# The feed-forward of an encoder layer as an up-pass and a down-pass through DRAM, with seven products down

## The chip, the core and the metric

The kernel runs on one core of a Trainium2 chip. The metric is the device time of one execution in microseconds, the median over runs. Times of single steps come from one profiled execution of the kernel before. The engines are TensorE (PE; its weight loads are listed as PEld), VectorE (DVE), ScalarE (ACT), GpSimd (POOL) and SyncE (SP), whose queue issues most of the DMA transfers.

## The reference, cut to what matters

One layer of a bidirectional encoder, applied to 2048 tokens of one request and 256 of another with the same weights, all in fp32. With D = 1024 and D_FF = 2816 the part that is changed is:

```python
x = x + concatenate([m_out, a_out], -1) @ w_out      # mixers: mLSTM heads, attention heads
h = rmsnorm(x, norm2_w)
u = centred_dwconv(h @ w_up, conv_w, conv_b)         # width 3 over positions, per channel
a, g = split(u, 2, axis=-1)                          # 2816 channels each
x = x + (silu(g) * a) @ w_down
y = rmsnorm(x, final_norm_w)
```

## The kernel before

Channels lie on the 128 partitions and tokens along the free dimension. The 2304 tokens of both requests are one row; the convolution is cut at token 2048. Phases a, b and c make the projections, the mixers and w_out; c stores x after the mixers in `x1_d` and its norm in `n2_d`, both in DRAM, and ends with the first up-products already under way. Phase d is the feed-forward.

A product in fp32 precision is made of three: each operand is split into a rounded part hi and a remainder lo (ScalarE copies hi, VectorE subtracts), and TensorE adds hi x hi, hi x lo and lo x hi in PSUM.

The up-projection is done by seven products for eight, in the Strassen-Winograd form: the weights of two channel tiles are a 2x2 matrix of quarters (`up_start`, names "11", "21", "t2", "t1", "t3", "22", "t4"), and so is the normed input of a token block (its halves of channels and of tokens, `n2_ops`). GpSimd forms the weights' sums (tw, lines 1189 to 1192); the inputs' sums are made by `n2_sums` (L1149) and put in DRAM as `n2t_d`, and `n2_load` brings the seven operands in and splits them. One call of `up` thus takes two channel tiles through seven products of 12 matmuls with up to 386 columns, into a PSUM bank each (p1, p2, p3, L1184), and u is put together by copies (ScalarE, L1200) and additions (VectorE, L1203).

Phase d loops over three blocks of 768 tokens, and in each over 11 groups of two channel tiles. A group calls `up` for the gate's two tiles and for the other branch's two. `conv` applies the width-3 convolution to each u (ScalarE L1271, VectorE L1278); five columns at a block's edge are carried over. The gate passes through silu, VectorE multiplies (L1358), and the result is split into act (L1363, L1364). Two tiles of w_down are loaded (rd, L1367) and split (wd, L1373, L1374). One group later `down` multiplies them by ordinary products: for eight channel tiles and two halves of 384 tokens, six matmuls (pd, L1322) into a bank, which VectorE adds to one of eight accumulators (L1324) that began as x. So each group's down-products lie among the next group's up-products. `finish` makes the final norm of a block: squares (ScalarE), their sums (GpSimd), rows of 1/rms by TensorE (L131, L142), a multiplication (L1312) and the store (L1313).

The order on each engine is laid out once, when the program is built, by a planner with a model of each instruction's time: an instruction is placed when its operands and a free buffer are there by the model, earlier ones in the program first. Each engine then goes through its list strictly in that order, and waits at the first instruction that isn't ready. The same holds for SP's and GpSimd's lists of DMA issues. Buffers of a tag are used in turn; a later pool in the same place waits for those instructions that used the tile that lay there.

Of the kernel before, what the change touches and what calls it, by code (L numbers as in the profile page):

```python
# [17 lines left out]
P = 128  # L18
D = 1024
# [16 lines left out]
BLK = 768  # L36
# [3 lines left out]
WU = 5  # L40
# [6 lines left out]
LAGO = 2  # L47
AB = 3
NH = 386
NW = 2 * NH + 1  # L50
DT = (0, 2 * NH, 2 * NH + BLK, T)
# [17 lines left out]
WD = 4  # L69
# [3 lines left out]
PO = 4  # L73
PB = 4
# [3 lines left out]
ZT = 3  # L78
SG = 3
RS = 2  # L80
# [914 lines left out]
def phase_c(g, sn, sp, pp, wps):  # L995
# [50 lines left out]
    def post(b, z, x, po, acc):  # L1046
        xz = x[:, 2 * z:2 * z + 2]
        nc.vector.tensor_tensor(xz, po, xz, ALU.add)
        if z % 2:
            g.st.dma_start(g.x1_d[b, :, 2 * z - 2:2 * z + 2], x[:, 2 * z - 2:2 * z + 2])  # L1050
# [26 lines left out]
    for n, b in enumerate(order):  # L1077
        x, mx = nxt
        for z in range(4):
# [14 lines left out]
            if n > 4 and sums:  # L1094

                n2_sums(g, sp, 0, sums.pop(0), tag="rn", bufs=2)
# [39 lines left out]
def n2_sums(g, pool, b, c, engs=("gpsimd",) * 4, tag="raw", bufs=RW):  # L1136


    nc = g.nc
    n = (DT[b + 1] - DT[b]) // 2  # L1140
    rs = []
    for k in range(2):
        r = pool.tile([P, D if tag == "raw" else 2 * NH], F32, tag=tag, name=f"rn{b}_{c}_{k}", bufs=bufs)[:, 0:2 * n]
        r = r.rearrange("p (h t) -> p h t", h=2)
        nc.sync.dma_start(r, g.n2_d[:, c + NCC // 2 * k, DT[b]:DT[b + 1]].rearrange("p (h t) -> p h t", h=2))
        rs.append(r)
    (b11, b12), (b21, b22) = ((r[:, 0], r[:, 1]) for r in rs)
    for eng, (o, p, q) in zip(engs, ((b11, b12, b11), (b12, b22, b12), (b22, b22, b11), (b21, b21, b22))):
        getattr(nc, eng).tensor_tensor(o, p, q, ALU.subtract)  # L1149
    for k in range(2):  # L1150
        g.st.dma_start(g.n2t_d[b, k, :, c, :, 0:n], rs[k])


def up_load(g, s1, b, jj):

    rs = [s1.tile([P, D], F32, tag="raw", name=f"ru{b}_{jj + k}", bufs=RW) for k in range(2)]
# [5 lines left out]
def up_start(g, s1, ps, ops, b, jj, rs=None):  # L1162
# [3 lines left out]
    n = (DT[b + 1] - DT[b]) // 2  # L1166
    nm = f"{b}_{jj}"
# [3 lines left out]
    t1, t2, t4 = (s1.tile([P, h], F32, tag="tmp", name=f"tw{k}_{nm}", bufs=3) for k in (1, 2, 4))  # L1171

    def bank(k):
        return ps.tile([P, 512], F32, tag="p", name=f"p{k}_{nm}", bufs=PB)[:, 0:n]

    def mul(p, k, src, add=False):

        w = s1.tile([P, 2, NCC // 2, P], F32R, tag="wu", name=f"wu{k}_{nm}", bufs=WU)
# [3 lines left out]
        for c in range(NCC // 2):  # L1182
            for i, (aa, bb) in enumerate(((0, 0), (0, 1), (1, 0))):
# [34 lines left out]
    return rest  # L1218


def phase_d(g, tc, s1, pd, ops, first):

    nc = g.nc
    ND = T // BLK
# [359 lines left out]
```

## Time and profile before

| | |
|---|---|
| median of 3 runs | 3429.08 us (3423.29 to 3429.88) |
| span of the profiled execution | 3427.2 us |
| TensorE busy | 3329.3 us, 97%, 20058 matmuls |
| VectorE, ScalarE, GpSimd busy | 2677.3, 1931.2, 1120.9 us |
| granted TensorE clock, mean | 0.990 |
| DMA, mean over the span | 118 GB/s, 404 MB |
| first up-product to last down-product | 1830 to 3411 us |

The median stands for the kernel; the profiled execution's own time is its span and the little that lies around it. A row of a group reads: line, engine, operation, tiles written and read, shape, number | busy time in us and mean ns of one | idle time of the engine just before them, with what ended it. A row of TensorE's timeline reads: start, duration of the run of like instructions, their kind and number. Matmuls overlap, so that their distance is read from start to start, not from their mean duration. A window row gives, after its length, the busy time of each engine with the number of its instructions, the granted clock, the DMA engines' busy share and their GB/s.

### The profile page before, as it was taken

To read this page: it belongs to the slowest core of one execution; us is meant where nothing else is said; L and a number is where in the kernel's file an instruction comes from. 1 tells how busy PE (TensorE), PEld (TensorE's weight loads), DVE (VectorE), ACT (ScalarE), POOL (GpSimd) and SP (SyncE) were. 2 spreads that over 40 slices of the span, in tenths; PEclk is the share of its full clock that TensorE was granted. 3 is DMA by queue.
4 is the path that set the end of the run, shared out by engine and by line. 5 is a ranking of instruction groups with operands and counts; after the bars stand their busy time and mean duration, and the time that the engine had idled before them with its cause. 6 is when DMAs were issued, how large, how long until landed. Compare 5 with 4: busy or idle time off the path is not lost. (4 is left out here: it accounts for less than half of the span.)

```text
span 3427.2 us, 55596 instructions
## 1 busy us (share of the span) xinstructions
PE 3329.3 (97%) x20058; PEld 3098.4 (90%) x20058; DVE 2677.3 (78%) x4654; ACT 1931.2 (56%) x4329; POOL 1120.9 (33%) x1328
## 2 busy tenths in 40 slices
PE   7989999999999999899999999999999999999998
PEld 6878888888888888688899999999999999999998
DVE  6885687777768788967767878789888888888776
ACT  4536666666666767655544444446444446555554
POOL 6653132213232323211244333226233224322222
PEclk9999999999999999999999999999999999999999
DMA  6765342333345444422365232223323213421221
GB/s 220 243 203 159 89 140 86 115 123 98 108 131 160 143 123 139 145 77 94 101 216 198 81 105 87 68 80 133 129 94 103 72 59 128 140 74 62 69 74 50
DMA packets 254756, 404.27 MB, mean 118 GB/s; under 512 B 32112, under 2 KB 156816, under 8 KB 254480
## 3 DMA queue, kind: packets, MB, share of 16 engines
q1 hardware_dynamic: 226576, 358.23, 32.7%
q0 software_dynamic: 11344, 33.04, 3.6%
q10 hardware_dynamic: 16560, 9.44, 0.9%
q8 instruction: 158, 2.59, 0.3%
q14 instruction: 118, 0.97, 0.1%
HBM read 316.73 MB, written 83.90 MB: 117 GB/s over the span
## 5 line engine op out<-in xcount | busy, mean ns | idle before, releaser
L1322 PE MATMUL pd<-act,wd 128*128 128x384 f32 (+1 forms) x3120 | 593.4, 336 | 23.9 <-DVE acc L1324 12.6
L1322 PEld LDWEIGHTS pd<-act,wd 128*128 128x128 f32 x3120 | 539.6, 188 | 32.6 <-DVE acc L1324 18.1
L601 DVE TENSOR_TENSOR pl<-ps,ph 128x512 fp32r<-128x512 f32 x520 | 352.7, 683 | 181.5 <-ACT ps L600 173.4
L1184 PE MATMUL pa<-nt,wut 128*128 128x386 f32 (+2 forms) x2376 | 454.3, 339 | 0.0
L599 ACT ACTIVATE ph<-ps 128x512 fp32r<-128x512 f32 x520 | 309.4, 595 | 243.5 <-PE ps L596 239.5
L1184 PEld LDWEIGHTS pa<-nt,wut 128*128 128x128 f32 x2376 | 421.6, 190 | 0.3 <-ACT u L1200 0.3
L570 DVE TENSOR_REDUCE mx<-px 128x1 f32<-128x512 f32 (+1 forms) x528 | 345.5, 670 | 74.4 <-PE px L569 72.4
L1278 DVE SCALAR_TENSOR_TENSOR y<-u,cw,y 128x768 f32<-128x768 f32 (+1 forms) x264 | 315.6, 1196 | 36.4 <-ACT y L1271 29.3
L1189 POOL TENSOR_TENSOR tw<-ru 128x512 f32<-128x512 f32 x66 | 94.1, 1425 | 732.5 <-DMA ru<-w_up 558.5
L613 PE MATMUL pv<-ph,v 128*128 128x512 f32 (+1 forms) x1040 | 319.4, 401 | 1.0 <-ACT ph L599 0.8
L600 ACT ACTIVATE ps<-ps 128x512 f32<-128x512 f32 x520 | 310.3, 597 | 0.0
L1200 ACT ACTIVATE u<-pa 128x386 f32<-128x386 f32 (+2 forms) x264 | 128.3, 486 | 320.9 <-PE pa L1184 320.7
L1324 DVE TENSOR_TENSOR acc<-pd,acc 128x384 f32<-128x384 f32 (+1 forms) x544 | 280.3, 535 | 35.5 <-PE pd L1322 34.1
L1041 PEld LDWEIGHTS po<-cmx,wo 128*128 128x128 f32 x1728 | 220.7, 191 | 8.2 <-DVE mmx L931 0.6
L1041 PE MATMUL po<-cmx,wo 128*128 128x256 f32 x1728 | 224.2, 284 | 0.4 <-DVE mmx L931 0.4
L595 PE MATMUL ps<-qq,kk 128*128 128x512 f32 x520 | 215.5, 416 | 4.2 <-DVE mx L570 2.4
L569 PE MATMUL px<-kk,qq 128*128 128x512 f32 (+1 forms) x528 | 202.8, 413 | 6.0 <-DVE mx L570 2.9
L596 PE MATMUL ps<-qm,kl 65*128 65x512 f32 x520 | 206.7, 399 | 0.0
L759 PE MATMUL mj<-mn,wm 128*128 128x256 f32 x1296 | 203.0, 289 | 2.8 <-ACT og L773 1.9
L759 PEld LDWEIGHTS mj<-mn,wm 128*128 128x128 f32 x1296 | 187.1, 193 | 19.8 <-ACT og L773 2.0
L769 PEld LDWEIGHTS mv<-wm,mn 128*128 128x128 f32 x1296 | 182.8, 190 | 18.4 <-ACT qb L765 2.5
L769 PE MATMUL mv<-wm,mn 128*128 128x256 f32 x1296 | 196.5, 285 | 1.0 <-ACT qb L765 0.9
(288 smaller groups left out, 7266.6 us busy)
## 6 DMA issues: line engine op xcount, KB each, us to landing
ru<-w_up SPq DMA_DIRECT2D x132, 512.0 KB, 3.4
mn<-n_d SPq DMA_DIRECT2D x216, 256.0 KB, 3.4
rd<-w_down SPq DMA_DIRECT2D x66, 512.0 KB, 3.6
n_d<-n1T SPq DMA_DIRECT2D x18, 1024.0 KB, 5.6
dm<-nm_d POOLq DMA_DIRECT2D x72, 256.0 KB, 4.1
mjn<-n_d SPq DMA_DIRECT2D x72, 256.0 KB, 3.3
mvn<-n_d SPq DMA_DIRECT2D x72, 256.0 KB, 3.1
q_d<-qz SPq DMA_DIRECT2D x18, 512.0 KB, 3.7
```

The source lines that it names most:

```text
L570: nc.vector.tensor_reduce(s.mx[:, t, z0:z0 + 1], ps[:, 0:w], AX.X, ALU.max)
L599: nc.scalar.activation(ph, ps, AF.Exp)
L600: nc.scalar.activation(ps, ps, AF.Exp)
L601: nc.vector.tensor_tensor(pl, ps, f32(ph), ALU.subtract)
L613: nc.tensor.matmul(s.pv[0:HD if k in (1, 3) else P, 0:N], v, p, start=(kp == 0 and k == 0), stop=(2 * kp + 2 == s.nk and k == 5))
L759: nc.tensor.matmul(pj[:, o], s.w[c][:, a, o * P:(o + 1) * P], nT[c][:, :, h, :], start=(c + o + k == 0), stop=(c == NCC - 1 and k == 2 and ...
L769: nc.tensor.matmul(pv[:, o], nT[c][:, o, a, :], s.w[c][:, h, 256:512], start=(c + o + k == 0), stop=(c == NCC - 1 and k == 2 and o == 1))
L1041: nc.tensor.matmul(po[:, o], wo[z // 2][c][:, a, n], mx[c][:, h, :], start=(c == 0 and k == 0), stop=(c == NCC - 1 and k == 2))
L1184: nc.tensor.matmul(p, w[:, aa, c, :], ops[k][:, c, bb, 0:n], start=c == 0 and i == 0 and not add, stop=c == NCC // 2 - 1 and i == 2, skip_ ...
L1278: nc.vector.scalar_tensor_tensor(y[:, s:e], u[:, s + k:e + k], cw[:, k, jj:jj + 1], y[:, s:e], ALU.mult, ALU.add)
L1322: nc.tensor.matmul(po, wds[j][c // 4][:, aa, c % 4 * P:(c % 4 + 1) * P], acts[j][:, bb, z0:z1], start=(j == 0 and k == 0), stop=(j == len( ...
L1324: nc.vector.tensor_tensor(accs[c][:, z0:z1], po, accs[c][:, z0:z1], ALU.add)
```

## The change

Phase d becomes two passes with the activations in DRAM between them.

**Up-pass (`phase_u`).** Two blocks of 1152 tokens instead of three of 768, with the same 11 groups. Operands and products are 572 or 580 columns wide in place of 382 to 386; each product is made in two halves (z) of 286 or 290 columns in two PSUM banks, so that one call of `up` has 7 x 24 matmuls. The weights' buffers are 4, not 5, and the raw weights lie in two pools. There are no down-products. The gated result of a group is a 2x2 matrix (two channel tiles by two halves of 576 tokens); GpSimd forms four sums (t1, t2, t3, t4) and stores all seven operands in `a_d` from its own DMA queue. `n2_sums` works in quarter pieces and through GpSimd's queue as well, in buffers shared with t1, t2 and t4.

**Down-pass (`phase_e`).** Seven products, each over 11 pairs of rows of w_down (p), for four tiles of 128 output channels (half of D) and 1152 columns (half of each block), in three column groups of 384 (z). For each product (i) and column group, TensorE goes through the 11 pairs with 12 matmuls each into two tiles of two PSUM banks; `update` copies or adds them to one or two of four accumulators (`quad`). Activations are loaded by fours of pairs in four buffers, and split; weights are loaded in two buffers (dw), split into 13 (w), and fetched during a product's last column group for the next product. The accumulators begin without x; x is loaded and added by GpSimd once an accumulator is nearly done (`resid`), and the norm's squares follow. The last product's last column group goes by halves of its channels.

Four of the seven weight operands are sums. GpSimd forms them inside the down-pass, in three buffers of their own (ds): t1 and t2 for all 11 pairs while the first product runs (`sums_a`: three loads, an addition, a subtraction, two stores to `s_d`), t3 and "22" while the second runs (`sums_b`: four loads, one of them of t2 from `s_d`, two subtractions, two stores). They are loaded again from `s_d` as weights. The loads are issued by SP, the stores by GpSimd.

`x1_d` is laid out by channel tile and token, and w_down is read once for the unsummed weights and again for the sums, not once per block.

```diff
-BLK = 768
+BLK = 1152
-WU = 5
+WU = 4
-NH = 386
+NH = 580
-DT = (0, 2 * NH, 2 * NH + BLK, T)
+DT = (0, 2 * NH, T)
+HB = BLK // 2
+TW = T // 2
+NP = NFC // 2
+CG = 384
+WR = 13
+TR = 4
+DS = 3
+TG = 4
+WA = 2
...
@@ up_start, mul
-        for c in range(NCC // 2):
-            for i, (aa, bb) in enumerate(((0, 0), (0, 1), (1, 0))):
-                nc.tensor.matmul(p, w[:, aa, c, :], ops[k][:, c, bb, 0:n], start=c == 0 and i == 0 and not add,
-                                 stop=c == NCC // 2 - 1 and i == 2, skip_group_check=add)
+        for z in range(2):
+            for c in range(NCC // 2):
+                for i, (aa, bb) in enumerate(((0, 0), (0, 1), (1, 0))):
+                    nc.tensor.matmul(p[:, z], w[:, aa, c, :], ops[k][:, c, bb, z * m:z * m + m],
+                                     start=c == 0 and i == 0 and not add, stop=c == NCC // 2 - 1 and i == 2,
+                                     skip_group_check=add)
...
@@ phase_u, a group
+            def store(k, gi, t):
+                nc.gpsimd.dma_start(g.a_d[gi // TG][DOPS.index(k), :, gi % TG, b * HB:(b + 1) * HB], t)
...
+                for y, yg in zip(yas, ygs):
+                    nc.vector.tensor_tensor(y, y, yg, ALU.mult)
+                b11, b12, b21, b22 = (y[:, k * HB:(k + 1) * HB] for y in yas for k in range(2))
+                store("11", gi, b11)
+                nc.gpsimd.tensor_tensor(t1, b12, b11, ALU.subtract)
+                nc.gpsimd.tensor_tensor(t2, b22, t1, ALU.subtract)
+                for k, t in (("t2", t2), ("21", b21), ("t1", t1)):
+                    store(k, gi, t)
+                nc.gpsimd.tensor_tensor(b12, b22, b12, ALU.subtract)
+                nc.gpsimd.tensor_tensor(t4, b21, t2, ALU.subtract)
+                for k, t in (("t3", b12), ("22", b22), ("t4", t4)):
+                    store(k, gi, t)
...
+def phase_e(g, tc, pd):
...
+        def halves(t, src):
+            lo, hi = t[:, 1], t[:, 0]
+            nc.scalar.activation(hi, src, AF.Copy)
+            nc.vector.tensor_tensor(lo, src, f32(hi), ALU.subtract)
...
+        def sums_a(p):
+            a, b = raw(0, 1, p, "ds", DS), raw(1, 1, p, "ds", DS)
+            nc.gpsimd.tensor_tensor(b, a, b, ALU.add)
+            nc.gpsimd.dma_start(g.s_d[SUM["t1"], p], b)
+            c = raw(0, 0, p, "ds", DS)
+            nc.gpsimd.tensor_tensor(c, b, c, ALU.subtract)
+            nc.gpsimd.dma_start(g.s_d[SUM["t2"], p], c)
+
+        def sums_b(p):
+            a, b = raw(0, 0, p, "ds", DS), raw(0, 1, p, "ds", DS)
+            nc.gpsimd.tensor_tensor(b, a, b, ALU.subtract)
+            nc.gpsimd.dma_start(g.s_d[SUM["t3"], p], b)
+            a, b = raw(1, 0, p, "ds", DS), saved("t2", p)
+            nc.gpsimd.tensor_tensor(b, a, b, ALU.subtract)
+            nc.gpsimd.dma_start(g.s_d[SUM["22"], p], b)
+
+        def weight(i, p):
+            k = DOPS[i]
+            w = sw.tile([P, 2, h], F32R, tag="w", name=f"we{k}_{p}", bufs=WR)
+            if k in SRC:
+                r = raw(*SRC[k], p, "dw", 2)
+            else:
+                r = sy.tile([P, h], F32, tag="dw", name=f"dw{k}_{p}", bufs=2)
+                nc.sync.dma_start(r, g.s_d[SUM[k], p])
+            halves(w, r)
+            return w
...
+        def acts(i, z, q):
+            p0, p1 = TS[q]
+            t = sx.tile([P, 2, TG, CG], F32R, tag="t", name=f"te{DOPS[i]}_{z}_{q}", bufs=TR)[:, :, 0:p1 - p0]
+            nc.sync.dma_start(f32(t[:, 1]), g.a_d[q][i, :, :, z * CG:(z + 1) * CG])
+            halves(t, f32(t[:, 1]))
+            return t
...
+        for i, k in enumerate(DOPS):
+            for z in range(G3):
+                ps = [banks(g, pd[(g.nbank + 1) // 2 % 2], f"e{k}_{z}_{m}")[:, :, 0:CG] for m in range(2)]
...
+                for p in range(NP):
+                    if p % TG == 0:
+                        fetch_t(1)
+                    mul(p, range(4))
+                    if i == 0 and z == 0 or z == G3 - 1:
+                        fetch_w(1)
+                    n = (i * G3 + z) * NP + p
+                    if i == 0 and n % 2 == 0 and n < 2 * NP:
+                        sums_a(n // 2)
+                    if i in (1, 2) and (n - G3 * NP) % 3 == 0 and n < 6 * NP:
+                        sums_b((n - G3 * NP) // 3)
+                    if late and p % 3 == 2:
+                        late.pop(0)()
+                while late:
+                    late.pop(0)()
+                for m in range(2):
+                    update(m)
```

More of the change, by code (lines that the diff above doesn't have):

```diff
@@ L1211, in rest @@
         mul(p1, "t3", a21, True)
-        copy(u22, p1)
-        add(u22, u22, u21)
+        add(u22, p1, u21)
         mul(p3, "22", t4, True)
@@ L1410, in body @@
         dram("mix_d", [NB, P, NCC, BT])
-        dram("x1_d", [NB, P, NCC, BT])
+        dram("x1_d", [P, NCC, T])
+        g.a_d = [dp.tile([7, P, min(TG, NP - p), TW], F32, name=f"a_d{p}") for p in range(0, NP, TG)]
+        dram("s_d", [4, NP, P, D // 2])
         dram("q_d", [NT, P, 8, P])
```

323 lines of the change are left out of this document (185 added, 138 removed).

## The prediction

> **What bounds the kernel now.** The page comes first, its busy times and its chain of waits, then the stretch that the change rewrites, which begins with the first product of the up-projection at 1830 us and whose last down-product ends at 3411 us.
>
> ```profile
> span 3427.2 us, 55596 instructions
> PE 3329.3 (97%) x20058; PEld 3098.4 (90%) x20058; DVE 2677.3 (78%) x4654; ACT 1931.2 (56%) x4329; POOL 1120.9 (33%) x1328
> PE pa L1184 12%; PE pd L1322 12%; PE pc L1184 6%; PE pb L1184 3%; DVE y L1278 1%; DVE acc L1324 1%; DVE wut L1181 1%; DMA ru<-w_up 1%; PE po L1041 1%; DVE wu L1181 1%; DMA rn<-n_d 1%; DVE act L1364 1%; DVE wd L1374 1%; DMA n2t_d<-rn 1%; DVE y L1358 1%
> ...
> core 0: us, PE busy (x) PEld busy (x) DVE busy (x) ACT busy (x) POOL busy (x), PEclk, DMA share, GB/s
> 1830.00:3411.00 1581.00, 1551.10 (x8898) 1540.74 (x8896) 1299.58 (x1796) 821.77 (x1629) 526.58 (x355) 1.00 0.28 93
> 3411.00:3428.00 17.00, 4.81 (x22) 4.08 (x20) 6.06 (x18) 3.51 (x10) 3.78 (x6) 0.58 0.36 125
> ```
>
> The chain of waits that ended last runs through the feed-forward's products pa, pb, pc (up) and pd (down). TensorE is busy for 1551 of those 1581 us at full clock. VectorE has 18% to spare, the DMA engines 72%. So the feed-forward is bound by TensorE, and its time is the number of matmuls times the distance between two starts, plus some 30 us of holes and a tail of 17 us. The groups give the numbers, TensorE's timeline the distances.
>
> ```profile
> L1322 PE MATMUL pd<-act,wd 128*128 128x384 f32 x2976 | 575.5, 339 | 23.9 <-DVE acc L1324 12.6 <-DVE act L1364 6.3 <-ACT act L1363 3.5
> L1322 PE MATMUL pd<-act,wd 128*128 128x256 f32 x144 | 17.9, 281 | 0.0
> L1322 PE MATMUL pd<-act,n 128*128 128x256 f32 x72 | 12.4, 284 | 0.0
> L1322 PE MATMUL pd<-nt,n 128*128 128x256 f32 x72 | 12.3, 280 | 0.0
> ...
> 1817.05 13.56 PE L1041 MATMUL po<-cmx,wo 128*128 128x256 f32 x111
> ...
> 2200.51 2.28 PE L1184 MATMUL pa<-nt,wut 128*128 128x386 f32 x12
> 2202.63 2.27 PE L1184 MATMUL pc<-nt,wut 128*128 128x386 f32 x12
> 2204.74 2.08 PE L1322 MATMUL pd<-act,wd 128*128 128x384 f32 x11
> 2206.66 2.30 PE L1184 MATMUL pa<-nt,wut 128*128 128x386 f32 x12
> ...
> L245 PE MATMUL pj<-w_a,n1T 128*128 128x288 f32 x24 | 3.3, 296 | 0.0
> ```
>
> A matmul lasts 0.34 us in the rows, but the next starts long before its end. From start to start: 386 columns 2.12/12 = 0.177 us; 384 columns 1.92/11 = 0.1745 us; 256 columns (13.56 - 0.28)/110 = 0.121 us; 288 columns, from a window in the first projection, (3.3 - 0.3)/23 = 0.130 us.
>
> **The change, part by part.**
>
> *Down-products.* Now 2976 matmuls of 384 and 288 of 256 columns: 519 + 35 = 554 us. With seven products: 7 x 11 row pairs x 4 column tiles x 3 halves' products x 3 column groups = 2772 of 384, 484 us. **-70 us.**
>
> *Up-products.* Two blocks instead of three, and each product is cut in two PSUM banks. Now 3 blocks x 22 x 7 x 12 = 5544 matmuls at 0.177 = 980 us; then 2 x 22 x 7 x 24 = 7392 of 286 or 290 columns. By the 288 row that is 7392 x 0.130 = 961 (-19); by a line through the 256 and 386 rows 0.1347 us, 996 us (+16). The line is measured on whole runs and at two widths, the 288 row is rounded to 0.1 us, so I stay between them, nearer to the line: 0.133 us, **+4 us** (-19 to +16).
>
> *Holes that go.* The down matmuls' 23.9 us of waiting in their row is for VectorE's accumulators and for the activations' splits; both lie worst at the two block changes:
>
> ```profile
> 2320.00:2355.00 35.00, 29.13 (x152) 27.54 (x151) 35.00 (x38) 17.75 (x32) 23.90 (x13) 0.95 0.33 105
> 2850.00:2945.00 95.00, 84.84 (x472) 83.25 (x471) 85.59 (x113) 58.24 (x118) 54.50 (x37) 0.96 0.36 119
> ```
>
> 6 and 10 us are lost there, with VectorE busy without a break in the first. The 544 accumulator additions (row L1324 below) become 42 wide ones. **-24 us.**
>
> *Holes that the up-pass gets.*
>
> ```profile
> L1324 DVE TENSOR_TENSOR acc<-pd,acc 128x384 f32<-128x384 f32 (+1 forms) x544 | 280.3, 535 | 35.5 <-PE pd L1322 34.1
> L1278 DVE SCALAR_TENSOR_TENSOR y<-u,cw,y 128x768 f32<-128x768 f32 (+1 forms) x264 | 315.6, 1196 | 36.4 <-ACT y L1271 29.3 <-ACT yc L1276 5.7
> L1271 ACT ACTIVATE y<-u,cw 128x768 f32<-128x768 f32 x132 | 134.8, 1021 | 33.9 <-DVE y L1358 31.2 <-DVE u L1203 2.5
> L1200 ACT ACTIVATE u<-pa 128x386 f32<-128x386 f32 x88 | 42.9, 487 | 101.9 <-PE pa L1184 101.8
> L1363 ACT ACTIVATE act<-y 128x768 fp32r<-128x768 f32 x65 | 54.7, 841 | 94.6 <-DVE y L1358 57.7 <-PE pd L1322 37.0
> L1364 DVE TENSOR_TENSOR act<-y,act 128x768 fp32r<-128x768 f32 x65 | 77.9, 1199 | 1.0 <-ACT act L1363 1.0
> L1373 ACT ACTIVATE wd<-rd 128x512 fp32r<-128x512 f32 x124 | 72.0, 618 | 9.1 <-PE pd L1322 9.0
> L1374 DVE TENSOR_TENSOR wd<-rd,wd 128x512 fp32r<-128x512 f32 x124 | 94.2, 779 | 0.0
> ...
> L1184 PE MATMUL pc<-n,wu 128*128 128x386 f32 (+2 forms) x792 | 153.7, 341 | 1.0 <-ACT u L1200 1.0
> L1184 PE MATMUL pc<-nt,wut 128*128 128x386 f32 (+2 forms) x792 | 151.7, 338 | 0.9 <-POOL nt L1129 0.9
> ...
> L856 POOL DMA_DIRECT2D dm<-nm_d x72: 536/607/659, 278.4 to 1406.8; - x72
> ```
>
> One block change is left, with operands 1.5 times as long and no down-product to run meanwhile: 10 us as in the longer of the two windows (3 to 20). At its start, four late operands of 1.5 times the size are awaited where 0.9 us is lost now: 4 us (0 to 15). In between I charge nothing. A product now lasts 24 x 0.133 = 3.2 us, which covers the evacuation of the bank it doesn't use (u, 0.49 us for 386 columns, so 0.74 for 580, behind at most one convolution step of 1.02 x 1.5 us). VectorE's conv steps (1196 ns for 768 columns) are 1.8 us for 1152; four of them, seven weight splits (0.8), three additions (0.8) and one product of the two branches (1.8) are some 17 of the 22.4 us of an up call. GpSimd gets, for each group of two calls, 4 sums of the activations beside its 8 of the weights (1.4 to 1.8 us for 512 columns, rows further down) and 7 DMA issues of 0.6 us: 25 of 45 us. **+14 us.**
>
> *The seam.* The down-pass's first activations are loaded where the last operands of the up-pass lay, its first weights where a u buffer lay. So after the last up matmul: either a load of 0.79 MB (7.0 us for 512 KB in the dense first stage, row below), a copy and a subtraction of 1536 columns (about 1.7 and 2.4 us), or the last convolution (0.7 + 1.5 + 3.6), a load (3.4, mn below) and a weight's splits (1.4). Both make 11 to 12 us; nothing else is there for TensorE: 12 us (8 to 20). Then the first eleven weights pass through two buffers, a load and two splits, 5.1 us, for each two, against 2 x 12 x 0.1745 = 4.2 us of matmuls: 6 us (0 to 13). **+18 us.**
>
> *The down-weights' sums*, the largest unknown. While the first two products run (2 x 3 x 11 x 12 x 0.1745 = 138 us), GpSimd forms 44 sums of 128x512 through three buffers: load, add, store to DRAM, and later the load again.
>
> ```profile
> q1 hardware_dynamic: 226576, 358.23, 32.7%
> ...
> mn<-n_d SPq DMA_DIRECT2D x216, 256.0 KB, 3.4
> dm<-nm_d POOLq DMA_DIRECT2D x72, 256.0 KB, 4.1
> n2t_d<-rn SPq DMA_DIRECT2D x8, 386.0 KB, 2.7
> ...
> x<-xT SPq DMA_DIRECT2D x16, 512.0 KB, 7.0
> mn<-n_d SPq DMA_DIRECT2D x24, 256.0 KB, 5.1
> ...
> L1191 POOL TENSOR_TENSOR ru<-ru,ru 128x512 f32<-128x512 f32 x64 | 112.5, 1757 | 0.0
> L1189 POOL TENSOR_TENSOR tw<-ru 128x512 f32<-128x512 f32 x64 | 91.5, 1430 | 729.2 <-DMA ru<-w_up 555.1 <-DVE acc L1324 114.7 <-DVE wu L1181 22.1
> ...
> 1738.53 2.44 SPq L1145 DMA_DIRECT2D rn<-n_d  x2
> 1749.84 0.32 SPq L1145 DMA_DIRECT2D rn<-n_d  x1
> ```
>
> (The second mn row is of the first 260 us, where the DMA engines move 223 GB/s.) In a round of the first kind a buffer is held for load + sum + store: at the least 3.4 + 1.4 + 2.7 = 7.5 us, at the most 5.1 + 1.8 + 4.1 plus waiting in line, some 12 us; the nearest thing in the trace, the rn rounds of load, subtractions and store through two buffers, starts anew after 11.3 us. I take 10.5 us, so eleven rounds 115 us. The last sum is wanted some 90 us after the start (69 for the first product, 21 into the second). **+25 us** (0 to 50). A second count agrees: in these 138 us 13 MB of activations (22 x 128 x 1152 x 4 bytes), 9.2 MB of weights (35 of 0.262 MB), and 14.4 and 17.3 MB for the sums (11 x 5 and 11 x 6 transfers) move, 54 MB; queue q1's row gives 358.23/(0.327 x 3427) = 320 GB/s at full engines, so 168 us, 30 more than TensorE needs.
>
> Here 256 KB land in 4.1 us from GpSimd's queue and in 3.4 us from SP's, and the sum above uses the 4.1. [...]
>
> *Norms and tail.* The norms take a single PSUM tile out of the pair rotation, so that the next column group's second tile waits for one addition, some 1 us (a bank pair's addition of 768 columns, twice the 0.54 us of row L1324): five times, +5 us (3 to 10). The tail keeps its squares, row sums, power, eight multiplications and stores, but leaves the last squares to TensorE's row sums, where GpSimd is now busy for 3.78 of the last 17 us: -3 us (0 to -4).
>
> Sum: -70 + 4 - 24 + 14 + 18 + 25 + 5 - 3 = **-31 us**. The profiled execution spans 3427.2 us, the median of the runs is 3429.1, 1.9 us around it. 3427.2 - 31 + 1.9 = 3398; I say **3400 us**, 0.8% less.
>
> **The rivals.** About 0.2%, 7 us, is what a measurement of this kernel can tell from no change.
>
> *The sums are hidden.* If the list of sums runs ahead of need, or its traffic spreads over the later products, where the DMA engines have room, the 25 us and most of the seam's 18 fall away: 3400 - 33 = 3367 us. For it: two of the four sums aren't used before the fourth and sixth product, and at 7.5 us a round the first kind is done in 83 us, before the 90. Against it: the 54 MB in 138 us need more than 320 GB/s.
>
> *SP's queue is tied to the sums* (slower). SP issues loads in a fixed order and waits at the head for a free buffer:
>
> ```profile
> SPq L1367 <- DVE wd L1374: 291.0, 32, 15.5
> ```
>
> It stood 9 us each time here, harmless as the loads are early. In the down-pass the loads of activations and weights stand behind the sums' loads. If the order was laid out for quick rounds, 22 rounds of 11.3 us take 249 us where TensorE needs 138; the activations in flight (three of four buffers) cover 25 us once. So 86 us instead of 25: 3461 us. It decides as soon as a round lasts more than (138 + 25)/22 = 7.4 us and the order puts each round ahead of the loads needed in its time; that the first half holds is likely, the second no row shows.
>
> *The up-pass alone has holes.* If each of the 44 up calls loses 1 us at a PSUM bank that the copy hasn't freed, 3444 us. Against it: 1.0 us of such waiting in the whole row of pc<-n,wu now, for 0.9 for the other, and 3.2 us of cover.
>
> **How the numbers follow.** Forecast 0.46 (own range 3382 to 3425, so 0.43 of it faster); hidden sums 0.21, faster; SP tied 0.22, of which 0.17 slower and 0.05 none to tell; holes in the up-pass 0.11, 0.07 slower. Faster 0.64, same 0.12, slower 0.24. The range reaches to the hidden case's better half and to the tied case: 3360 to 3461.
>
> **What would show it.** TensorE's distance for 290 columns at 0.130 to 0.135 us and for the down-products 0.1745; 7392 and 2772 of them. A hole of about 12 us before the first down-product. In the first two down-products, holes of together 25 us ended by weights (w) that came from the summed DRAM tiles; none in the last four beyond the norms. If the holes are ended by activations or by weights that are no sums, SP was tied. If TensorE's busy time falls by less than 60 us, the matmul prices were wrong, and with them the forecast.

## The result, and the profile after

| | before | changed |
|---|---|---|
| median | 3426.78 us (4 runs) | 3455.87 us (3452.22 to 3459.66, 4 runs) |
| ratio, 95% interval | 1 | 1.0086 [1.0072, 1.0101] |
| span of the profiled execution | 3427.2 us | 3454.7 us |
| TensorE busy, matmuls | 3329.3 us, 20058 | 3284.3 us, 21402 |

The change makes the kernel 0.9% slower. 3400 us was forecast; the time lies in the range (3360 to 3461), on the wrong side of the kernel before. The page of the changed kernel, in the same parts as before:

```profile
span 3454.7 us, 57226 instructions
PE 3284.3 (95%) x21402; PEld 3050.8 (88%) x21402; DVE 2469.8 (71%) x3748; ACT 1774.1 (51%) x3702; POOL 1427.5 (41%) x1651
PE pa L1197 7%; PE et L1478 5%; PE pc L1197 4%; PE pb L1197 2%; DMA ds<-w_down 2%; DMA s_d<-ds 2%; PE e L1478 1%; DMA te<-a_d 1%; DMA dst<-s_d 1%; DVE y L1295 1%; DMA dw<-w_down 0%; POOL ds L1362 0%; POOL ds L1370 0%; DVE we L1345 0%; POOL sm L1429 0%
L1478 PE MATMUL et<-tet,wet 128*128 128x384 f32 x1584 | 285.3, 340 | 15.4 <-ACT wet L1344 11.0
L1043 PE MATMUL po<-cmx,wo 128*128 128x256 f32 x1728 | 224.2, 284 | 25.0 <-DVE cx L1050 24.6
L1478 PE MATMUL e<-te,we 128*128 128x384 f32 x1188 | 215.7, 341 | 27.5 <-ACT we L1344 21.2
```

TensorE is busy for 45 us less, but the span is 27.5 us longer. The chain of waits now has DMA transfers in it that weren't there: the loads and stores of the sums (ds, s_d). The last three rows name three places where TensorE stands: a product of w_out in phase c (po, 25 us), and down-products with unsummed (e, 27.5) and summed weights (et, 15.4). The windows show where, first of the kernel before in the 40 us ahead of its up-products, then of the changed one:

```profile
1790.00:1830.00 40.00, 39.34 (x331) 39.14 (x330) 22.58 (x44) 10.45 (x21) 16.57 (x13) 1.00 0.57 189
```

```profile
1790.00:1830.00 40.00, 14.75 (x104) 14.32 (x103) 17.71 (x25) 9.82 (x16) 17.98 (x21) 0.70 0.88 280
1830.00:1881.00 51.00, 38.13 (x310) 37.30 (x308) 14.97 (x29) 9.27 (x13) 14.52 (x13) 0.90 0.45 145
1881.00:2885.00 1004.00, 987.25 (x7318) 983.95 (x7319) 827.89 (x658) 506.10 (x842) 610.18 (x474) 0.99 0.32 108
2885.00:2906.00 21.00, 1.71 (x7) 1.48 (x6) 15.30 (x12) 9.96 (x13) 4.82 (x6) 0.56 0.64 215
2906.00:3175.00 269.00, 245.55 (x1342) 239.02 (x1342) 108.08 (x84) 72.80 (x81) 117.85 (x106) 0.96 0.76 257
3175.00:3441.00 266.00, 258.44 (x1491) 257.48 (x1489) 137.83 (x139) 73.48 (x72) 81.35 (x45) 0.98 0.50 162
```

The 1004 us of the up-pass and the last 266 of the down-pass are nearly dense. Most of the time goes in the 91 us around phase c's end, in the 21 us between the passes, and in the 269 us of the first products of the down-pass. TensorE's timeline has the holes (in brackets: idle time before, and what ended it):

```profile
1798.53 2.79 PE L1197 MATMUL pb<-n,wu 128*128 128x290 f32 x19
1825.93 19.49 PE L1043 MATMUL po<-cmx,wo 128*128 128x256 f32 x149 [24.61 <-DVE cx L1050]
...
1862.82 3.39 PE L1197 MATMUL pa<-nt,wut 128*128 128x290 f32 x24
1867.40 0.61 PE L133 MATMUL rs_c<-ones,cacc 128*128 128x2 f32 x4 [1.19 <-POOL cacc L1059]
1869.11 0.71 PE L144 MATMUL rs_c<-ident,rcol_c 128*128 128x128 f32 x4 [1.10 <-POOL rcol_c L137]
1880.12 0.61 PE L1197 MATMUL pc<-nt,wut 128*128 128x290 f32 x1 [10.30 <-ACT nt L1130]
...
2878.79 3.34 PE L1197 MATMUL pc<-n,wu 128*128 128x286 f32 x24
2881.97 3.33 PE L1197 MATMUL pa<-nt,wut 128*128 128x286 f32 x24
2904.59 8.90 PE L1478 MATMUL e<-te,we 128*128 128x384 f32 x41 [19.29 <-ACT we L1344]
```

SP's timeline at the same places (the time at which a load or store left):

```profile
1795.72 0.33 SPq L1165 DMA_DIRECT2D ru<-w_up  x1
1810.32 3.57 SPq L1067 DMA_DIRECT2D n_d<-cx  x4
1816.97 6.00 SPq L1034 DMA_DIRECT2D cx<-xT  x4
...
1871.54 1.93 SPq L1067 DMA_DIRECT2D n_d<-cx  x2
1873.64 2.69 SPq L1129 DMA_DIRECT2D nt<-n2t_d  x4
...
2885.33 3.12 SPq L1392 DMA_DIRECT2D te<-a_d  x4
2901.42 0.81 SPq L1349 DMA_DIRECT2D dw<-w_down  x2
```

SP issues nothing from 1796 to 1810, then four stores of normed tokens (n_d<-cx), and only behind them the x of phase c's next block, for which TensorE stands 24.6 us. What SP waited for between 1795 and 1881, and in the first products of the down-pass (2880 to 3180):

```profile
SPq L1067 <- DMA rn<-n_d: 15.0, 3, 10.6
```

```profile
SPq L1349 <- DMA s_d<-ds: 68.6, 27, 5.6
SPq L1349 <- DMA s_d<-dst: 32.9, 9, 5.4
SPq L1349 <- DVE y L1295: 12.2, 1, 12.2
```

At 1796 a store of normed tokens waits for GpSimd's loads (rn) of the inputs' sums. They read other tokens of the same DRAM tensor `n2_d`: no data passes between the two. In the down-pass SP stands 101 us for the stores of the sums, whose three buffers it wants to load again, and 12 us for the last convolution's u, which lay where the first weights go.

### The profile page after: what moved, and what is told of

Read it like the earlier page. It is cut to its first block, busy times and chain, and to the rows that moved or that the text cites. A ratio compares the mean times of both kernels' runs of the same rounds, so it can differ in the third digit from the quotient of the medians.

```text
span 3454.7 us, 57226 instructions
## 1 busy us (share of the span) xinstructions
PE 3284.3 (95%) x21402; PEld 3050.8 (88%) x21402; DVE 2469.8 (71%) x3748; ACT 1774.1 (51%) x3702; POOL 1427.5 (41%) x1651
## 5 line engine op out<-in xcount | busy, mean ns | idle before, releaser
L1197 PE MATMUL pa<-nt,wut 128*128 128x290 f32 (+1 forms) x3168 | 448.9, 298 | 5.5 <-ACT u L1215 4.5
L1197 PEld LDWEIGHTS pa<-nt,wut 128*128 128x128 f32 x3168 | 433.8, 191 | 6.9 <-ACT u L1215 5.4
L572 DVE TENSOR_REDUCE mx<-px 128x1 f32<-128x512 f32 (+1 forms) x528 | 345.3, 670 | 73.6 <-PE px L571 71.4
L1295 DVE SCALAR_TENSOR_TENSOR y<-u,cw,y 128x1152 f32<-128x1152 f32 (+1 forms) x176 | 338.3, 1922 | 25.4 <-ACT yc L1293 12.1
L1478 PE MATMUL et<-tet,wet 128*128 128x384 f32 x1584 | 285.3, 340 | 15.4 <-ACT wet L1344 11.0
L1478 PEld LDWEIGHTS et<-tet,wet 128*128 128x128 f32 x1584 | 279.1, 191 | 19.4 <-ACT wet L1344 12.4
L1043 PE MATMUL po<-cmx,wo 128*128 128x256 f32 x1728 | 224.2, 284 | 25.0 <-DVE cx L1050 24.6
L1478 PE MATMUL e<-te,we 128*128 128x384 f32 x1188 | 215.7, 341 | 27.5 <-ACT we L1344 21.2
L1478 PEld LDWEIGHTS e<-te,we 128*128 128x128 f32 x1188 | 210.9, 192 | 30.8 <-ACT we L1344 22.0
L615 PE MATMUL pv<-pl,v 128*128 128x512 f32 x520 | 190.5, 399 | 0.0
```

The source lines that it names most:

```text
L572: nc.vector.tensor_reduce(s.mx[:, t, z0:z0 + 1], ps[:, 0:w], AX.X, ALU.max)
L615: nc.tensor.matmul(s.pv[0:HD if k in (1, 3) else P, 0:N], v, p, start=(kp == 0 and k == 0), stop=(2 * kp + 2 == s.nk and k == 5))
L1043: nc.tensor.matmul(po[:, o], wo[z // 2][c][:, a, n], mx[c][:, h, :], start=(c == 0 and k == 0), stop=(c == NCC - 1 and k == 2))
L1197: nc.tensor.matmul(p[:, z], w[:, aa, c, :], ops[k][:, c, bb, z * m:z * m + m], start=c == 0 and i == 0 and not add, stop=c == NCC // 2 - 1 ...
L1295: nc.vector.scalar_tensor_tensor(y[:, s:e], u[:, s + k:e + k], cw[:, k, jj:jj + 1], y[:, s:e], ALU.mult, ALU.add)
L1478: nc.tensor.matmul(ps[m // 2][:, m % 2], w[:, aa, m * P:(m + 1) * P], t[:, bb], start=p == 0 and n == 0, stop=p == NP - 1 and n == 2)
```

## The experiments

| run | edit | median, us | ratio to before, 95% interval |
|---|---|---|---|
| e1 | `n2_d` as two tensors | 3439.23 | 1.0032 [1.0022, 1.0043] |
| e2 | no sums | 3424.67 | 0.9982 [0.9973, 0.9991] |
| e3 | e1 and e2 | 3401.55 | 0.9919 [0.9901, 0.9936] |
| e4 | e1, sums in the up-pass | 3421.10 | 0.9974 [0.9963, 0.9985] |
| e5 | e4, places of late operands | 3418.95 | 0.9973 [0.9962, 0.9983] |
| e6 | e4, places of the down-pass | 3422.90 | 0.9988 [0.9978, 0.9997] |
| e7 | e4, late loads in GpSimd's queue | 3410.94 | 0.9949 [0.9934, 0.9964] |
| e8 | e5, e6, e7 | 3415.57 | 0.9962 [0.9949, 0.9975] |
| e9 | e7, places and order at the seam | 3395.84 | 0.9916 [0.9902, 0.9930] |
| e10 | e9, four raw weight buffers | 3397.83 | 0.9916 [0.9904, 0.9929] |
| e11 | e9, sums in the down-pass again | 3425.52 | 1.0002 [0.9992, 1.0012] |
| e12 | e11, sums' loads in GpSimd's queue | 3434.47 | 1.0017 [1.0007, 1.0028] |
| e13 | e11, six buffers for the sums | 3385.24 | 0.9879 [0.9863, 0.9894] |
| e14 | e12, six buffers for the sums | 3408.02 | 0.9944 [0.9932, 0.9957] |
| e15 | the changed kernel, six buffers | 3425.98 | 0.9997 [0.9988, 1.0006] |

### The store that waits for loads of other tokens, and the sums (e1 to e4)

e1 cuts `n2_d` at the token where the blocks part, so that stores of the second block touch another tensor than the loads of the first:

```diff
-        dram("n2_d", [P, NCC, T])
+        g.n2_d = [dp.tile([P, NCC, DT[k + 1] - DT[k]], F32, name=f"n2_d{k}") for k in range(2)]
```

> Changed kernel, but n2_d is two DRAM tiles, cut at token 1160, where the two blocks of the up-pass meet. Theory A (false wait): in the changed kernel the stores of the sixth token block's norm stand in SP's list behind GpSimd's loads for the input sums, which read the same DRAM tile but other tokens; SP waits from 1796 to 1810 us, the next x is loaded late, and TensorE stands still for 24.6 us. With two tiles the stores wait for nothing: 20 to 28 us faster than the changed kernel, 3428 to 3436 us. Theory B (the sums themselves are late): the hole moves to the first product with a summed operand, whose last sums are stored at 1821 us in any case: 0 to 8 us faster, 3448 to 3456.

e2 leaves the four sums out (`sums_a`, `sums_b`); the summed weights are replaced by an unsummed quarter of w_down:

```diff
-                    if i == 0 and n % 2 == 0 and n < 2 * NP:
-                        sums_a(n // 2)
-                    if i in (1, 2) and (n - G3 * NP) % 3 == 0 and n < 6 * NP:
-                        sums_b((n - G3 * NP) // 3)
```

> Changed kernel without the down-weights' sums: the four summed operands are replaced by an unsummed quarter of w_down, so the down product isn't computed rightly; loads, splits and matmuls of the down-pass stay. Theory S (the sums bind the first two products): the holes of the first 270 us of the down-pass are theirs, 25 to 35 us faster, 3421 to 3431. Theory W (the weights' two buffers and the DMA latency bind): the holes stay, 0 to 10 us faster, 3446 to 3456.

e3 has both edits.

> Both of the above: two DRAM tiles, and no down-weights' sums (the down product is not computed rightly). If the two holes are independent, the gains add up: with A and S 45 to 63 us faster than the changed kernel, 3393 to 3411; with B and W 0 to 18.

e4 has e1's edit and makes the sums in the up-pass's second block, one pair of rows in each of its 11 groups, in the buffers of t1, t2 and t4, with loads and stores in GpSimd's queue:

```diff
+            def wsums(p):
+                ...
+                nc.gpsimd.tensor_tensor(w11, w01, w11, ALU.add)
+                nc.gpsimd.dma_start(g.s_d[0, p], w11)
+                ...
             for gi, gr in enumerate(groups):
+                if b == ND - 1:
+                    wsums(gi)
```

> Two DRAM tiles for n2_d, and the down-weights' sums made by GpSimd in the second block of the up-pass, one row pair per group, through the three buffers of the activations' sums, with 4 loads and 4 stores on GpSimd's queue instead of 7 and 4. With theories A and S, and GpSimd's 46% of idle time there as cover: 40 to 60 us faster than the changed kernel, 3396 to 3416, and faster than the kernel before. If GpSimd's list is delayed by waits for its own DMA transfers, the up-pass loses 0.5 to 2 us in each of 11 groups, 5 to 20 us of it.

Since e2 and e3 leave sums out, they don't compute the layer. Against the changed kernel's 3455.9, e1 gains 16.6 us, e2 31.2 and e3 54.3: more than the sum of the two. The first hole is gone in e1; TensorE's timeline there, at phase c's end:

```profile
1812.46 7.95 PE L1043 MATMUL po<-cmx,wo 128*128 128x256 f32 x65
...
1847.87 0.71 PE L144 MATMUL rs_c<-ident,rcol_c 128*128 128x128 f32 x4 [0.75 <-POOL rcol_c L137]
1860.20 0.61 PE L1200 MATMUL pc<-nt,wut 128*128 128x290 f32 x1 [11.63 <-ACT nt L1133]
```

So the wait for tokens that were never shared is shown as the cause of the 24.6 us. The hole of 10.3 us behind it stays, and is 11.6 here. e4, which computes everything, lies 34.8 us below the changed kernel and is 0.3% faster than the kernel before. It stays 19.6 us above e3: the sums aren't free in the up-pass either, whose last product starts at 2875.41 us in e4 and at 2857.91 in e3.

### The late operands at the start of the up-pass (e5, e7)

e5 only changes the order in which the late operands' places are taken:

```diff
-        late = n2_ops(sl, 0, ("t4", "t1", "t3", "22"))
+        late = n2_ops(sl, 0, ("t4", "22", "t1", "t3"))
```

> e4 with one more edit: the four late operands' places are ordered t4, 22, t1, t3 (t1, the first one used, then no longer lies over the last norm's accumulator, so its load waits for no GpSimd instruction). Theory P (the place holds the load back): the first late load leaves SP at about 1838 instead of 1849.7 us, the hole of 11.0 us in front of the first product on it falls to 3 to 4, and the time is 3411 to 3415. Theory Q (SP's list is what holds it back: the last norm's two stores stand ahead of it, and they leave at 1847.5): the load leaves at 1849 to 1850 as in e4, the hole stays at 10 to 12 us, and the time is 3419 to 3423.

e7 keeps the places and puts the eight loads in GpSimd's queue:

```diff
-            n2_load(g, late, 0, k, engs=e)
+            n2_load(g, late, 0, k, engs=e, q="gpsimd")
```

> e4 with one more edit: the eight loads of the late operands stand in GpSimd's queue instead of SP's; their places are as in e4. Theory Q (SP's list): they pass the last norm's stores and leave at 1844 to 1845 us, right behind GpSimd's power of that norm, the hole falls from 11 to 6 to 7 us, the time is 3416 to 3418. Theory P (place): as in e4, since t1's place is let go only by that norm's last instruction; the hole stays at 9 to 12 us, the time is 3419 to 3423. Both agree that without the power's wait it would be shorter still.

SP's timeline in e5:

```profile
1849.80 1.93 SPq L1070 DMA_DIRECT2D n_d<-cx  x2
1851.89 3.40 SPq L1132 DMA_DIRECT2D nt<-n2t_d  x4
```

The place made no difference: e5's time is e4's within 2.2 us. The loads stand in SP's list behind the last norm's stores, and leave 2.1 us after them, as in e4 (1847.50 and 1849.73). In e7 TensorE's hole is half as long:

```profile
1850.13 0.71 PE L144 MATMUL rs_c<-ident,rcol_c 128*128 128x128 f32 x4 [0.76 <-POOL rcol_c L137]
1855.92 0.61 PE L1200 MATMUL pc<-nt,wut 128*128 128x290 f32 x1 [5.08 <-ACT nt L1133]
```

and the time falls by 10.2 us, 4 more than this hole gave back (11.04 us in e4). The traces show where the 4 us lie: from 1856 to 2340 us TensorE does 3546 matmuls in e7 and 3512 in e4, 34 x 0.135 = 4.6 us more work in the same time. Why the first block runs denser is not shown; each edit also makes the planner lay out all lists anew, so that differences of a few us can come from elsewhere.

### The seam between the passes (e6, e8, e9, e10)

e6 places the raw weights' and the operands' buffers over the up-pass's early operands:

```diff
+        sb = st.enter_context(tc.tile_pool(name="e_b", bufs=1, reuse_waits="tile"))
+        ... dw ...
+        sx = st.enter_context(tc.tile_pool(name="e_t", bufs=1, reuse_waits="tile"))
+        ... te ...
         sw = st.enter_context(tc.tile_pool(name="e_w", bufs=1, reuse_waits="tile"))
```

> e4 with one more edit: in the down-pass the two buffers of raw down-weights and the four of its operands are placed first, over the up-pass's early operands, and not behind the accumulators, over the buffers of its last convolutions. Theory M (the 19 us hole between the passes is a wait for a place in SBUF): the first weight load leaves SP 13 to 16 us earlier, the hole shrinks to 4 to 7 us, the time is 3405 to 3410. Theory L (the hole is the latency of load, copy and subtraction behind the last products, whatever the place): the hole stays above 15 us and the time is 3418 to 3422.

e8 has the edits of e5, e6 and e7.

> e4 with the edits of e5, e6 and e7 together. If the place and the list each hold the late operands back and lifting one alone uncovers the other, the late loads leave at 1834 to 1838 us, that hole is 1 to 4 us, and with the seam at 4 to 7 us the time is 3395 to 3402 (e4 less 8 less 13). If the hole in front of the late operands is set by the sums of the normed tokens, whose last round ends at 1828, or by the splits into high and low parts behind the loads, it stays at 8 to 11 us and the time is that of e6.

e6 is no faster than e4, and e8 is 4.6 us above e7 alone. TensorE's and then ScalarE's timeline in e6:

```profile
2895.90 5.55 PE L1506 MATMUL e<-te,we 128*128 128x384 f32 x22 [15.90 <-ACT we L1372]
...
2908.09 4.29 PE L1506 MATMUL e<-te,we 128*128 128x384 f32 x12 [4.17 <-ACT we L1372]
```

```profile
2894.66 0.66 ACT L1302 ACTIVATE y<-u,yc,cw 128x1 f32<-128x1 f32 x2 [5.74 <-DVE y L1298]
2895.24 0.61 ACT L1372 ACTIVATE we<-dw 128x512 fp32r<-128x512 f32 x1
```

SP had issued the first weights' loads much earlier:

```profile
2860.99 0.82 SPq L1377 DMA_DIRECT2D dw<-w_down  x2
```

Yet the copy of the first (we<-dw) stands in ScalarE's list behind two one-column corrections of the last convolution, which wait for VectorE. The hole went from 19.1 to 15.9 us, and a second of 4.2 us followed. The buffer's place was one lock; the order in the lists was the next. e9 opens both, on top of e7: residuals' buffers too over early operands, the accumulators over the convolution's, and the first fetch ahead in the planner's order:

```diff
-        fetch_w(WA)
-        fetch_t(2)
+        with tc.high_priority(offset=MPRI):
+            fetch_t(1)
+            fetch_w(WA)
+        fetch_t(1)
```

> e7 with a seam edit that reaches further than e6's: the raw weights', residuals' and operands' buffers of the down-pass lie over the up-pass's early operands, the split weights over its late ones, the accumulators over the convolution's buffers; and the first operand and the first two weights are given a high priority, so that their copies stand ahead of the last convolution's end in ScalarE's and VectorE's lists. Theory I (in e6 the hole stayed at 16 us since the copy of the first weight stood behind the last convolution on ScalarE): the first down-product starts 3 to 7 us after the last up-product instead of 19, a second hole of 2 to 6 us follows at the third weight, and the time is 3398 to 3404 (e7's 3411 less 7 to 13). Theory J (ScalarE and VectorE owe the last group's convolution and the first splits some 18 us of work whatever the order, and what is done first only moves the hole): the first hole falls, but together the holes of the first 60 us of the down-pass stay within 4 us of e7's, and the time is 3407 to 3412.

```profile
2873.21 0.62 PE L1510 MATMUL e<-te,we 128*128 128x384 f32 x2 [2.63 <-ACT we L1374]
2875.33 6.98 PE L1510 MATMUL e<-te,we 128*128 128x384 f32 x24 [1.51 <-DVE te L1375]
```

TensorE's timeline in e9: 19.1 us have become 2.6 and 1.5. The time falls by 15.1 us against e7. e10 has more raw buffers on top, and its time is e9's within 2 us:

```diff
-            sb.tile([P, h], F32, tag="dw", name=f"place_dw{k}", bufs=2)
+            sb.tile([P, h], F32, tag="dw", name=f"place_dw{k}", bufs=4)
```

> e9 with four buffers of raw down-weights instead of two. If the first weights of the down-pass are held by the round trip of a raw buffer (load some 2 us, copy, subtraction, free again), this takes 2 to 5 us from e9; if by ScalarE's and VectorE's lists, it is e9 within 2 us.

This is no clean test of the buffers: in e10's trace the first weight's copy (we) again comes late on ScalarE, with a hole of 14.2 us in front of the first down-product, while the up-pass happens to end 4.9 us earlier. A raw weight's load, expected at some 2 us, landed in 2.9 us in e4 (median of 19, 2900 to 3180). From the start of the last up-product to the start of the last 38 matmuls of the down-pass it is 507 us in e10, 503 in e9 and 516 in e7.

### What the sums cost in the down-pass (e11 to e15)

e11 is e9 with the sums where the change has them: e4's `wsums` is gone, `sums_a` and `sums_b` are back.

> e9 with the down-weights' sums left where the change has them, in the first products of the down-pass, in their own buffers: what the sums cost there once the waits of the other parts are mended. Theory S (the sums' own price, by GpSimd's rounds and the loads in SP's queue): 3412 to 3422, e9 plus 13 to 20, as the changed kernel with own tiles stood 18 to 38 above the variants with the sums in the up-pass or left out. Theory T (the sums cost little; what they showed was the seam's waits made longer): e9 plus 0 to 6.

It is 29.7 us slower than e9, more than either theory gave: the price is the sums' own. In the down-pass it is larger still. The sums had cost e9 17 us in the up-pass, whose last product starts at 2867.25 us there and at 2850.24 in e11; from that start to the start of the last 38 down-products it is 503 us in e9 and 549 in e11. In e12 their loads are taken off SP's queue:

```diff
-            nc.sync.dma_start(r, g.w_down[0, ...])
+            (nc.gpsimd if tag == "ds" else nc.sync).dma_start(r, g.w_down[0, ...])
```

> e11 with one more edit: the sums' own loads, of raw down-weights and of the one saved sum, stand in GpSimd's queue instead of SP's; the sums, their buffers and their place in the first products are as in e11, and so are the bytes. Theory V (SP's list is tied to the sums: the loads of the products' own weights and activations stand behind the sums' loads, and these wait at the head of the queue for the store of the round before): TensorE's stalls in the first products fall, and the time is 3397 to 3407, 19 to 29 below e11. Theory R (the transfers' rate: the sums raise the stretch from some 150 to 250 GB/s and each transfer lands later): 3418 to 3428 as e11. In between, both.

It is not faster but 9 us slower. SP's longest waits there, from 2860 to 3200 us, are for summed weights that are to be loaded (L1393), and none is for the sums' buffers, whose loads it no longer issues:

```profile
SPq L1393 <- DMA s_d<-ds: 124.1, 16, 12.5
```

So the list of SP alone is not the cause, and the rate of the transfers or the pace of a round were left. e13 and e14 double the buffers at the same bytes, at the price of one split weight:

```diff
-WR = 13
-DS = 3
+WR = 12
+DS = 6
```

> e11 with six buffers for the sums instead of three and twelve for the split weights instead of thirteen. In e11 SP's loads for a round wait for the stores of the round before (81 us in 28 waits). If this pace (load, add, store, load into the same buffer) is what the sums cost: rounds overlap, the stalls of the second product fall by half or more, the time is 3400 to 3412, 14 to 26 below e11. If it is the rate of the transfers or the one weight buffer less: 3420 to 3432.

> e12 with the same six and twelve buffers: the sums' loads are in GpSimd's queue. If e12 lost by the pace of the rounds alone (its second product waited 35 us in eight waits for summed weights), the rounds are now quicker and SP's queue is free of them: 3396 to 3408. If by the rate: 3420 to 3435.

Windows of the second product in e11, and then in e13:

```profile
2950.00:3025.00 75.00, 64.20 (x336) 61.41 (x335) 31.50 (x24) 17.23 (x19) 25.90 (x26) 0.94 0.73 243
```

```profile
2950.00:3025.00 75.00, 75.00 (x435) 75.00 (x433) 40.96 (x31) 21.49 (x24) 39.94 (x38) 1.00 0.97 335
```

e13 is 40.3 us below e11. With 335 GB/s in place of 243 TensorE is full: the rate was a consequence of the rounds, not their limit. e13 even beats e9, where the sums lie in the up-pass, by 10.6 us: its last up-product starts 15 us earlier, and from there on it takes 506 us against 503. e14 gains 26 against e12, and stays 23 above e13: with six buffers SP's queue was the better one. The last run makes these two constants the only edit of the changed kernel.

> The changed kernel with two constants changed and nothing else: six buffers for the sums instead of three, twelve for the split weights instead of thirteen. If the three buffers are what the sums cost in the changed kernel too: as e2, which left the sums out, 3422 to 3430, some 25 to 34 below the changed kernel's 3455.9 and no slower than before. If the price came with the waits at the seam, which this leaves as they are: 3440 to 3452.

It is 29.9 us faster than the changed kernel, and level with the kernel before. The first sum of each round in the changed kernel from 2905 to 2990 (number: shortest, median and longest ns, first and last start), and in e15 from 2885 to 2990:

```profile
L1362 POOL TENSOR_TENSOR ds<-ds,ds x7: 1278/1286/2678, 2909.4 to 2981.6; 128x512 f32<-128x512 f32 x7
```

```profile
L1362 POOL TENSOR_TENSOR ds<-ds,ds x11: 1273/1284/1679, 2910.2 to 2983.8; 128x512 f32<-128x512 f32 x11
```

A round takes 72.2/6 = 12.0 us through three buffers, and 73.6/10 = 7.4 us through six. (Over all eleven rounds of t1 and t2, whose last starts at 3020.5 in the changed kernel, it is 11.1 us; the rounds of t3 and "22" take 12.7 us, in e15 7.6.) The windows of the first 269 us, in e15:

```profile
2900.00:3169.00 269.00, 266.13 (x1511) 263.77 (x1512) 135.13 (x100) 83.74 (x92) 124.54 (x108) 0.99 0.79 272
```

1511 matmuls where the changed kernel had 1342: 169 x 0.1724 = 29 us. That is the gain within a few us (the hole at the seam is 16.0 us long here, not 19.3). The sums now cost next to nothing: e2, which left them out, has a median 1.3 us lower, and by the two ratios it is some 5 us faster, with intervals that just overlap. From the start of the last up-product to the start of the last 38 down-products it is 551 us in the changed kernel, 518 in e15 and 520 in e2.

## Why the prediction was wrong

*Matmuls: right.* 290 columns take (3.39 - 0.29)/23 = 0.135 us, 286 columns (2881.97 - 2878.79)/24 = 0.1325, 384 columns 75/435 = 0.1724; 0.133 and 0.1745 were used. The counts, 7392 and 2772, came out. By these distances the up-products are some 5 us dearer than forecast and the down-products some 6 us cheaper. The text wanted TensorE's busy time to fall by 60 us, or the matmul prices were wrong. It fell by 45, and they weren't: e13 has the same matmuls and is busy for 3267.5 us, 62 less than before. So the same matmuls were busy for 16.8 us more in the changed kernel, at a mean granted clock of 0.978 against e13's 0.987, and this was a bad test.

*The step that failed* is a term that the sum puts at nothing. The part on what is moved prices the down-weights' sums, but not the sums of the inputs at the end of phase c. The change makes these 1.5 times as long, cuts them in halves, moves them to GpSimd's queue and needs a fifth token block before they can start; so they run on into the stretch where SP stores the next blocks. The wait of those stores left TensorE idle for 24.6 us, against nothing in the sum. e1 shows it; taken alone it gave back 16.6 us, and 23.1 with the sums of the weights left out (e3 against e2). In e1 the last up-product starts 19.0 us earlier, but the down-pass with its waits for sums is 3.9 us longer.

*Holes that the up-pass gets.* The start was 4 us (0 to 15): measured are the holes of 1.19, 1.10 and 10.30 us and the first product's short ones. The size of the operands was seen, but not that their loads stand behind the norm's stores in SP's list (e5, e7). The block change was 10:

```profile
2362.00:2410.00 48.00, 37.77 (x259) 35.96 (x257) 45.89 (x27) 27.40 (x37) 34.75 (x15) 0.96 0.53 186
2410.00:2885.00 475.00, 472.26 (x3549) 471.80 (x3550) 370.13 (x319) 250.19 (x464) 252.63 (x198) 0.99 0.26 91
```

These windows of the changed kernel give 48 - 259 x 0.1325 = 14 us, and 475 - 3549 x 0.1325 = 5 us for the rest of the block: so the block change took 4 us more than forecast. In between nothing was charged; 5 us were lost there, and 481 - 3512 x 0.135 = 7 us in the first block (1881 to 2362). At 12 us instead of 44 the rival of a lost us in every up call falls.

*The seam:* 12 us (8 to 20) were forecast, 19.3 measured. Two ways of 11 to 12 us each were counted as if side by side. They share ScalarE, VectorE and their lists, as e6 and e9 show, and so come one after the other. That the part as a whole was near (18 us) is luck: its other 6 us, for the first weights through two buffers, aren't there. In e2, without the sums, a single wait of 0.7 us follows behind that hole, up to 3165 us.

*The down-weights' sums:* 25 us (0 to 50) were forecast, 30 measured. The size was near, the working half right. A round was taken at 10.5 us and takes 11 to 12.7. Of the 23 us of holes in the first products of the changed kernel (2908 to 3200), 13 are ended by summed weights and 10 by unsummed weights and activations, which the prediction named as a sign that SP is tied to the sums: by that sign it was so in part. The second count (54 MB at 320 GB/s, so 30 us too many) agreed by chance: e13 moves 335 GB/s in the second product with TensorE full.

*Norms and tail.* One norm's wait of 6.8 us stands in the place of five of 1 us; the tail is 13.7 us long, 16.2 before (from 3411 to 3427.2): -3, as said.

*The rivals.* "SP's queue is tied to the sums" gave 3461 us, and the time was 3456; but its 86 us for the sums are not what happened, and e12 refutes that SP's list by itself is the cause. Its condition, that it decides when a round lasts more than 7.4 us, isn't contradicted: at 11 to 12.7 us the sums cost 30 us, at 7.4 to 7.6 next to nothing. Where between these the price begins, no run shows. "The sums are hidden" is what e15 shows, with 7.5 us a round as its text asked; the SBUF for it was there, with the thirteenth weight buffer given up.

*GpSimd's stores.* The forecast let them land in 4.1 us. In the changed kernel (2906 to 3175) the stores of the sums landed in 4.1 and 5.3 us (ds, dst) and SP's loads into the same buffers in 3.6 and 4.2: 0.5 and 1.1 us more, and no run shows the reason. In e13's window of 335 GB/s they land as soon as SP's loads do (list of transfers: number, KB each, median us to landing), so the delay isn't seen there:

```profile
ds<-w_down SPq DMA_DIRECT2D x28, 256.0 KB, 6.1
...
s_d<-ds POOLq DMA_DIRECT2D x11, 256.0 KB, 6.0
```

By lengths of holes and misses of terms, with the other terms as forecast, the change lost 24.6 us at the end of phase c, 8.6 more than forecast at the start of the up-pass, 4 at the block change, 12 in between, 1 at the seam, 5 by the sums and 2 by the norm: 57 of the 58.5 us between the -31 forecast and the 27.5 measured. The edits say the same less exactly. e15's is worth 29.9 us, e1's 16.6, e7's 10.2, e9's 15.1: 71.8 together, and e13, which has all four, lies 70.6 below the changed kernel. That these agree so well is chance, for the edits aren't independent: without the buffers the other three give 30.4 us together (e11), and the buffers then 40.3. The forecast of 3400 less its own 25 us for the sums would be 3375; e13 reaches 3385.

## What to carry to other kernels

Ask of every in-order list which instruction stands at its head when its wait is long, and what other work stands behind it: here four waits for things that the work behind didn't need (a DRAM tensor's other tokens, a norm's stores, a convolution's last columns, a buffer's store) made most of the way from -31 to +27 us. Price a chain of load, sum and store by its round and the number of its buffers: here a round took 12.0 us through three and 7.4 through six, at the same bytes, so that a count of bytes by itself said little. When a plan moves work, list all that it moves, also what serves the next stage, before pricing the part that looks new.

## What the runs showed of the hardware

A stretch with holes lost more than their length. In the first of these windows of 75 us of the same product, in the changed kernel, TensorE is idle for 9.5 us and makes 89 matmuls fewer than in the second, 89 x 0.1724 = 15.3 us:

```profile
2950.00:3025.00 75.00, 65.54 (x346) 63.03 (x345) 27.66 (x17) 19.67 (x21) 34.65 (x32) 0.93 0.71 240
3025.00:3100.00 75.00, 75.00 (x435) 75.00 (x434) 32.75 (x30) 19.56 (x22) 22.03 (x23) 1.00 0.77 260
```

A matmul takes 65.54/346 = 0.189 us of busy time in the first and 0.172 in the second: the granted clock was 0.93 against 1.00. Windows of 75 us in other runs have 71.69/403 = 0.178 at 0.97 (e11, from 3025), 70.83/394 = 0.180 at 0.95 and 66.41/365 = 0.182 at 0.93 (e14, from 3100 and 2950). An estimate from the full window, with the time inverse to the clock, is 0.172/0.97 = 0.178 and 0.172/0.93 = 0.185; by it the clock makes up most of the difference, and what the rest is, the windows don't show. The granted clock was 0.56 in the 21 us of the seam, where TensorE is busy for 1.71 us, and 1.00 in the window in which it is full.

A load of the sums landed in 6.1 us at 335 GB/s (e13, above) and in 3.6 at 257 (the changed kernel, 2906 to 3175); through six buffers the rounds were quicker all the same (7.3 us in e13, nine first sums from 2890.6 to 2949.0, against 12.0 in the changed kernel).
